# A greedy planner's allowances: results counted later for the transfers that read them, and a margin of 0.44 for TensorE in place of 0.42

## The chip, the cores and the metric

The kernel runs on one core of one Trainium2 chip. Its time is the device time of one execution in microseconds (us). A core has five engines with a line of instructions each: TensorE (PE, with its weight loads listed apart as PEld), VectorE (DVE), ScalarE (ACT), GpSimdE (POOL) and SyncE (SP), which here issues every DMA transfer. An engine takes its instructions in the order in which they were issued and waits on semaphores for the others.

## What is computed

One step of a hybrid decoder layer for 1024 new tokens of a prompt and 8 sample tokens with states of their own, model width 1024:

```python
p = x @ w_in                                   # 9360 columns: GLA, RWKV-7 and gate parts
o_gla, S_gla = gla_chunked(q, k, v, log_a)     # 4 heads, 128 x 256 state
o_gla = rmsnorm(o_gla) * silu(g_a)
pr = p_rwkv + (prev - p_rwkv) * mu             # token shift
y, S_rwkv = rwkv7_scan(r, w, k, v, kk, a)      # 16 heads, 64 x 64 state, one step per token
o_rwkv = (groupnorm(y) + bonus) * silu(g_b)
m = sigmoid(gate_a) * (o_gla @ w_up_gla) + sigmoid(gate_b) * (o_rwkv @ w_up_rwkv)
y_out = layernorm(alpha * x + m @ w_out)
```

Outputs are y for both groups, the new GLA and RWKV states, and the last projected RWKV rows. All is float32; the large matmuls are made from a high and a low part of each operand, three products each.

## The kernel before

**Stages.** The tokens go in two passes of 512 (the 8 sample tokens ride with the first). In each pass every block of 128 columns of `w_in` is projected: eight blocks of 128 rows by three products, for one or two tiles of tokens. From these rows come four GLA heads (`gla_head`) and eight pairs of RWKV heads (`pair`: `front`, `back`, `turn`, `chain`, `norm`). A pair's `front` makes Gram matrices, stores parts of them to DRAM (`LD`), loads them back in another layout, solves triangular blocks on VectorE (tiles `X`), and stores and reloads the result (`XD`, `XT`, `Xs`). A pair's `chain` is serial over eight chunks: three small matmuls (`pch`) with copies and scaled additions between them, and one pair's chain starts only when the one before has ended. Late in the second pass the eight sample states (`rwkv_sample`, loads `row<-state_rwkv`, stores `rwkv_s<-row`) are worked through. Then come the up projections with the gates (stored before as `sg`, loaded again by `load_gates`, merged as `mg`), and the output projection with the layer norm.

**Weights.** `load_w` loads a half block (`wraw`), ScalarE casts the high part into `wb`, VectorE or GpSimdE subtracts the low part, and in the first pass the split tile is also stored to DRAM (`keep`, `w<-wb`), from where the second pass loads it (`wb<-w`). There are four `wb` tiles. In `load_w`'s `low`, the tile is handed to the matmuls (`self.ws.append`) after the store has been issued.

**The order of issue.** Nothing of the order is written by hand. The work is written as some dozens of generators (`Stream`s), each of which yields its operations one at a time. `Order.run` is a greedy planner that runs while the program is built: at each step it asks every stream for its next operation, estimates when that could start (`start`), takes off a priority by the kind of stream, and issues the operation with the smallest key. It keeps an account of each engine's time, of when each tile is ready and by which engine it was made, and of when it was last read. The program that results is fixed; at run time the engines follow it with semaphores. So the constants of the estimate change the order of instructions, and nothing else.

In `start`, an operation can begin when its engine is free and when each of its tiles is ready. If another engine made a tile, an allowance is added: `HOP` for the maker, and `SPARE` more if the reader is TensorE and the maker VectorE, ScalarE or GpSimdE. `HOP["D"]` is for tiles that a transfer filled. If the same engine made it, 0.13 us are added (not for TensorE). A transfer (engine "S") costs SyncE 0.48 us in the account; `transfer` gives its time in the DMA engines, bytes of all runs divided over 16 engines at 0.01 us and 46.5 ps per byte a run, and 1.7 us (1.2 to DRAM) until it has landed. Only one operation of a stream is open at a time, so a stream whose transfer is planned later goes on later.

Of the kernel before, what the change touches and what calls it, by code (L numbers as in the profile page):

```python
# [20 lines left out]
P = 128  # L21
D = 1024
# [39 lines left out]
OUT_AHEAD = 3  # L62


HOP = {"P": 0.2, "D": 1.7, "G": 0.14, "V": 0.15, "A": 0.14}

SWITCH = 0.115
HOLD = 0.11
# [1 line left out]

AGE = 0.5

SPARE = 0.42
BIAS = 0.1
ASIDE = 0.5

# [164 lines left out]
class Order:  # L241
# [89 lines left out]
    def start(self, op):  # L331

        best = None
        for eng, fn, cost in op.ways:
            free, t = self.time[eng] + (SWITCH if eng == "P" and op.tiles != self.tiles else 0.0), 0.0
            for x in (op.out, *op.ins):
                at, by = self.ready.get(x.tensor.name, (0.0, None))
                if eng == "S" and by == "D" and x is op.out:
                    continue
                if by != eng:  # L340
                    at += HOP.get(by, 0.0) + (SPARE if eng == "P" and by in ("V", "A", "G") else 0.0)
                elif eng != "P" and x is not op.out:
                    at += 0.13
                t = max(t, at)
            t = max(t, self.read.get(op.out.tensor.name, 0.0))
            if eng in op.port:
                free = max(free, self.port["G" if eng == "V" else "V"])
            late, t = free - t, max(t, free)
            if eng in "VA" and self.held(eng, op):
                cost += HOLD  # L350
            end = t + cost
            if len(op.ways) > 1:
                end += BIAS if eng == "V" and "A" in op.ways[0][0] else ASIDE if eng == "G" and "G" in op.port else 0.0
            if best is None or end < best[0]:
                best = end, t
                op.eng, op.fn, op.cost, op.late = eng, fn, cost, max(0.0, late)
        return best[1]
# [1441 lines left out]
```

## Time and profile before

| | |
|---|---|
| runs | 1514.95, 1516.04, 1519.06 us; median 1516.04 |
| profiled execution | 1520.49 us, span 1518.7 us |
| granted TensorE clock, mean | 0.997 |
| TensorE busy | 1481.2 us (98%) |
| VectorE, ScalarE, GpSimdE busy | 1125.9 (74%), 877.4 (58%), 94.5 (6%) |
| DMA | 330.58 MB, 69.7% of 16 engines' span |

The span is the time from the first to the last instruction in the trace. "Idle before, releaser" in the rows of the profile is how long an engine stood before an instruction and whose result ended that; a row of the waits has the total in us, the number of times and the longest. All instructions carry the line 219, where a helper records them, so they are told apart by the names of their tiles (`out<-in`). In the rows by stretches of time, each engine's busy time is followed by its number of instructions, then come the granted clock, the share of the DMA engines that was busy and GB/s.

### The profile page before, as it was taken

The page shows a single profiled execution, that of the slowest core. Times are in us where ns is not written, and L with a number is a line of the kernel's source. Part 1 is how long each engine was busy: PE and PEld are TensorE (multiplying, and loading weights), DVE is VectorE, ACT ScalarE, POOL GpSimd, SP SyncE. Part 2 cuts the span into 40 slices and gives each one's busy share as a digit, 9 for nine tenths or more (in the row PEclk, how much of TensorE's full clock was granted, in tenths as well). Part 3 has the DMA queues.
Part 4 walks back from the last instruction along what each step waited for, and adds up shares of the span by engine and source line. Part 5 has one row for each costly group of instructions (what it writes and reads, how often), then busy time and mean ns, then how long its engine had stood idle before and what let it go on. Part 6 is the DMA issues. An engine that isn't in the chain of part 4 may idle for free.

```text
span 1518.7 us, 31506 instructions
## 1 busy us (share of the span) xinstructions
PE 1481.2 (98%) x11352; PEld 1303.4 (86%) x11352; DVE 1125.9 (74%) x2570; ACT 877.4 (58%) x2209; POOL 94.5 (6%) x273
## 2 busy tenths in 40 slices
PE   8999999999999999999999999899999999999997
PEld 7999999999999998877878777778788899988786
DVE  5687789786986698669778888776765775665665
ACT  5666677675677577566664555456546645554310
POOL 1010000000110000001001010200000000000000
PEclk9999999999999999999999999999999999999999
DMA  8768977789768976586576557555764778697622
GB/s 305 259 226 263 308 259 220 221 245 308 238 210 251 309 249 218 175 245 178 162 199 209 148 164 234 170 142 176 200 194 127 217 241 260 238 312 252 208 84 83
DMA packets 252823, 330.58 MB, mean 218 GB/s; under 512 B 125011, under 2 KB 148700, under 8 KB 252668
## 3 DMA queue, kind: packets, MB, share of 16 engines
q1 hardware_dynamic: 252668, 328.58, 69.7%
q8 instruction: 90, 1.47, 0.4%
q14 instruction: 65, 0.53, 0.1%
HBM read 198.35 MB, written 118.61 MB: 209 GB/s over the span
## 4 chain that ended last, share of the span: by engine, by line
PE 74%; DVE 13%; DMA 6%; ACT 3%; issue 2%; SPq 1%; POOL 0%; POOLq 0%; DVEq 0%; ACTq 0%
PE proj L219 45%; PE big L219 16%; PE pY L219 8%; DVE row L219 6%; PE pch L219 5%; DVE X L219 3%; ACT row L219 2%; SPq L219 1%; DVE wide L219 1%; DMA row<-sg 1%; DMA wide<-LD 1%; DVE part L219 1%; DMA w<-wb 1%; DVE pair L219 1%; DMA row<-state_rwkv 0%
## 5 line engine op out<-in xcount | busy, mean ns | idle before, releaser
L219 PE MATMUL proj<-xh,wb 128*128 128x256 f32 (+3 forms) x3744 | 912.7, 328 | 1.1 <-DVE row L219 0.8
L219 PEld LDWEIGHTS proj<-xh,wb 128*128 128x128 f32 x3744 | 624.4, 189 | 46.5 <-issue 2.6
L219 PE MATMUL proj<-xl,wb 128*128 128x256 f32 (+3 forms) x1872 | 612.1, 327 | 0.0
L219 PEld LDWEIGHTS proj<-xl,wb 128*128 128x128 f32 x1872 | 353.8, 189 | 23.2 <-issue 1.9
L219 DVE TENSOR_TENSOR wb<-wraw,wb 128x512 fp32r<-128x512 f32 x208 | 141.9, 689 | 78.1 <-ACT wb L219 74.3
L219 ACT CAST wb<-wraw 128x512 fp32r<-128x512 f32 x210 | 129.9, 622 | 90.3 <-PE proj L219 41.1
L219 DVE TENSOR_TENSOR row<-row 128x512 f32<-128x512 f32 (+8 forms) x338 | 166.1, 501 | 15.3 <-DMA row<-state_rwkv 6.4
L219 ACT ACTIVATE row<-row 128x512 f32<-128x512 f32 (+3 forms) x229 | 138.6, 611 | 36.2 <-DVE row L219 17.7
L219 DVE SCALAR_TENSOR_TENSOR wide<-pch,pc,s0p 64x64 f32<-64x64 f32 x224 | 63.1, 281 | 51.9 <-PE pch L219 46.9
L219 PE MATMUL big<-row 128*128 128x128 f32 (+4 forms) x466 | 87.1, 322 | 9.0 <-DVE row L219 4.1
L219 ACT ACTIVATE row<-proj,omu 128x256 f32<-128x256 f32 (+1 forms) x99 | 54.2, 548 | 68.6 <-PE proj L219 67.6
L219 ACT COPY rh<-pch 128x128 f32<-128x128 f32 x118 | 31.4, 266 | 105.6 <-PE pch L219 104.3
L219 DVE TENSOR_REDUCE X<-X 128x54 f32<-128x162 f32 (+14 forms) x256 | 85.4, 334 | 6.4
L219 ACT ACTIVATE s0p<-wide,pc 64x64 f32<-64x64 f32 x256 | 88.9, 347 | 1.8
L219 POOL TENSOR_TENSOR row<-row 128x256 f32<-128x256 f32 (+6 forms) x47 | 42.5, 909 | 688.0 <-DVE row L219 435.6
L219 DVE SCALAR_TENSOR_TENSOR row<-proj,pv,row 128x255 f32<-128x255 f32 (+1 forms) x99 | 56.4, 570 | 35.3 <-ACT tail L219 25.4
L219 PEld LDWEIGHTS big<-row 128*128 128x128 f32 (+3 forms) x466 | 59.5, 178 | 21.1 <-ACT row L219 7.0
L219 DVE TENSOR_TENSOR X<-X,wide 128x108 f32<-128x108 f32 (+14 forms) x256 | 71.2, 278 | 6.6
L392 ACT ACT_TABLE_LOAD x58 | 74.4, 1283 | 1.0
L219 PE MATMUL big<-xh,wb 128*128 128x512 f32 (+2 forms) x272 | 69.2, 332 | 2.9 <-ACT wb L219 2.6
L219 ACT COPY row<-big 128x128 f32<-128x128 f32 (+5 forms) x145 | 43.3, 317 | 38.4 <-PE big L219 35.5
L219 PE MATMUL pY<-xh,wb 128*128 128x256 f32 (+2 forms) x256 | 63.2, 326 | 0.0
(269 smaller groups left out, 2324.8 us busy)
## 6 DMA issues: line engine op xcount, KB each, us to landing
w<-wb SPq DMA_DIRECT2D x146, 512.0 KB
wb<-w SPq DMA_DIRECT2D x146, 512.0 KB
wraw<-w_in SPq DMA_DIRECT2D x146, 256.0 KB
wide<-LD SPq DMA_DIRECT2D x64, 128.0 KB
wraw<-w_up_gla SPq DMA_DIRECT2D x32, 256.0 KB
wraw<-w_up_rwkv SPq DMA_DIRECT2D x32, 256.0 KB
sg<-row SPq DMA_DIRECT2D x16, 260.0 KB
row<-sg SPq DMA_DIRECT2D x16, 260.0 KB
```

Of the source, the lines that this page charges most:

```text
L219: ways.append((eng, lambda call=call: call(out, *args, **kw), price(eng, name, out, args, ins)))
L392: self.nc.scalar.preload_act_table_set(self.table)
```

## The change

Three constants of the planner's estimate. VectorE's hop is 0.14 in place of 0.15, TensorE's margin on results of other engines is 0.44 in place of 0.42, and a transfer now has such a margin too (`STORE`, 0.3) on tiles that VectorE, ScalarE or GpSimdE made. No operation is added, removed or altered.

```diff
-HOP = {"P": 0.2, "D": 1.7, "G": 0.14, "V": 0.15, "A": 0.14}
+HOP = {"P": 0.2, "D": 1.7, "G": 0.14, "V": 0.14, "A": 0.14}
...
-SPARE = 0.42
+SPARE = 0.44
+STORE = 0.3
 BIAS = 0.1
 ASIDE = 0.5
...
                 if by != eng:
-                    at += HOP.get(by, 0.0) + (SPARE if eng == "P" and by in ("V", "A", "G") else 0.0)
+                    at += HOP.get(by, 0.0) + (SPARE if eng == "P" and by in ("V", "A", "G") else STORE if eng == "S" and by in ("V", "A", "G") else 0.0)
                 elif eng != "P" and x is not op.out:
                     at += 0.13
                 t = max(t, at)
```

## The prediction

> **What bounds the kernel now.** I read the page first, then the busy time by stretches of 50 us, then the waits of TensorE and of the DMA queue, then the timeline at the places where TensorE stood longest.
>
> ```profile
> span 1518.7 us, 31506 instructions
> PE 1481.2 (98%) x11352; PEld 1303.4 (86%) x11352; DVE 1125.9 (74%) x2570; ACT 877.4 (58%) x2209; POOL 94.5 (6%) x273
> ```
>
> TensorE is busy for 1481.2 of 1518.7 us. Whatever the order of issue does, the matmuls are the same ones, so the whole sum that another order can win from idle time is 1518.7 − 1481.2 = 37.5 us, less what is idle at the two ends. The stretches show where it lies:
>
> ```profile
> core 0: us, PE busy (x) PEld busy (x) DVE busy (x) ACT busy (x) POOL busy (x), PEclk, DMA share, GB/s
> ...
> 750.00:800.00 50.00, 48.51 (x311) 38.93 (x310) 39.10 (x103) 30.68 (x71) 3.64 (x4) 1.00 0.78 226
> 800.00:850.00 50.00, 47.04 (x339) 37.76 (x338) 44.45 (x116) 20.96 (x63) 8.16 (x17) 1.00 0.59 167
> 850.00:900.00 50.00, 47.85 (x327) 38.27 (x328) 42.21 (x81) 33.08 (x84) 5.05 (x13) 1.00 0.56 162
> 900.00:950.00 50.00, 48.80 (x307) 39.17 (x305) 41.57 (x92) 26.70 (x59) 1.34 (x2) 1.00 0.77 228
> 950.00:1000.00 50.00, 45.24 (x319) 36.52 (x320) 39.38 (x99) 20.25 (x62) 9.26 (x17) 0.97 0.59 167
> ...
> 1200.00:1250.00 50.00, 47.14 (x376) 43.91 (x375) 34.97 (x79) 27.45 (x53) 1.32 (x1) 0.97 0.76 230
> ...
> 1500.00:1518.70 18.70, 10.92 (x71) 9.74 (x69) 10.35 (x19) 0.99 (x4) 2.77 (x3) 0.92 0.17 61
> ```
>
> The last stretch loses 18.70 − 10.92 = 7.8 us in the closing normalisation, which has no other work beside it in any order. From 750 to 1000 us TensorE loses 250 − 237.44 = 12.6 us and around 1225 us another 2.9; only in the stretches that hold 950 and 1225 us is the granted clock below 1.00. Who ended these waits:
>
> ```profile
> PE pch L219 <- DVE wide L219: 4.6, 5, 2.0
> PE big L219 <- DVE row L219: 4.1, 6, 2.0
> PE big L219 <- DVE part L219: 3.5, 5, 1.4
> PE big L219 <- ACT wb L219: 2.6, 1, 2.6
> PE pch L219 <- ACT wide L219: 2.6, 3, 1.5
> ...
> PE proj L219 <- DVE wb L219: 0.2, 1, 0.2
> ```
>
> These are the first five and the last of 21 rows (total us, times, longest). All 21 add up to 28.9 us in 41 waits: 29 ended by VectorE, 10 by ScalarE, 2 by a transfer. They are the stock on which the change can work. The DMA queue's own waits:
>
> ```profile
> SPq L219 <- PE proj L219: 217.1, 100, 7.5
> SPq L219 <- DVE wb L219: 111.5, 80, 6.5
> SPq L219 <- DVE row L219: 88.1, 78, 5.5
> SPq L219 <- DVE X L219: 87.5, 53, 7.5
> ```
>
> SyncE issues every transfer in one line. It stands for 217.1/100 = 2.17 us at a time until matmuls let go of a buffer that a load will fill, and for 1.1 to 1.7 us at a time until VectorE has made what a store reads. Such time costs nothing by itself; it costs if a transfer that somebody needs is queued behind.
>
> **Part 1: TensorE's margin.** Nothing that runs is added or taken out; all three edits alter what the order of issue believes. For an operand made by VectorE the allowance becomes 0.14 + 0.44 = 0.58 in place of 0.15 + 0.42 = 0.57 us; made by ScalarE or GpSimdE, 0.58 in place of 0.56. A wait that a planned start 0.01 or 0.02 us later would shorten is shorter by just that: 29 × 0.01 + 10 × 0.02 = 0.5 us at most. On the other side, TensorE takes a projection matmul first a little more often, and a step of the serial chains is planned that much later. That costs nothing while projections fill the gap, which 98% busy says they do; without that cover the 16 pairs × 8 chunks × 3 matmul steps of the chain would be up to 384 × 0.02 = 7.7 us. I take −0.5.
>
> **Part 2: VectorE's hop.** ScalarE and GpSimdE now plan on VectorE's results 0.01 us sooner. ScalarE is 58% busy and GpSimdE 6%, so this prices at nothing; if ScalarE's order filled up it would be 0.01 us for each such operand, of which none shows among TensorE's waits. I take 0.
>
> **Part 3: the stores.** A transfer that reads a result of VectorE is planned 0.14 + 0.30 − 0.15 = 0.29 us later, one that reads ScalarE's or GpSimdE's 0.30. Two things follow: loads that are ready in that time are issued ahead of the store, and what follows the store (its landing, and the reads of what it wrote) is expected 0.3 us later, so more other work is put before it. The largest family is the copy of the split weights to DRAM in the first pass.
>
> ```profile
> L219 SPq DMA_DIRECT2D w<-wb x146: 320/448/1545, 6.5 to 580.0; - x146
> ```
>
> ```profile
> 126.86 1.47 PE proj L219 x12
> ```
>
> The stream that makes the weights hands a tile on only when this store has been issued, so in the planner's time each of 146 tiles is 0.29 us later. One tile feeds 24 matmuls, 24 × 1.47/12 = 2.9 us, and there are four tiles, so 11.8 us of matmuls hide it; the wait on this source in the table above is 0.2 us. With the cover gone it would be 146 × 0.29 = 42 us, and nothing in the first pass is near that. Zero.
>
> What can be won lies where a late transfer shows through to TensorE. I find three such places. The first is the start of the up projections:
>
> ```profile
> 1216.15 0.50 SPq L219 DMA_DIRECT2D row<-sg  x1
> ```
>
> ```profile
> 1222.14 0.64 ACT L219 ACTIVATE row<-row 128x520 f32<-128x520 f32 x1 [3.06 <-DMA row<-sg]
> ...
> 1230.36 0.39 PE L219 MATMUL big<-xh,wb 128*128 128x256 f32 x1 [2.64 <-ACT wb L219]
> ...
> 1231.09 0.51 PE L219 MATMUL big<-xh,wb 128*128 128x256 f32 x2 [0.22 <-DVE wb L219]
> ```
>
> The reader of a gate load starts 1222.14 − 1216.15 = 6.0 us after its issue, ScalarE idles 3.06 us for it with the casts of the next weights behind, and TensorE pays 2.64 + 0.22 = 2.86 us. The second and third are loads of the sample states:
>
> ```profile
> 943.37 0.69 DVE L219 TENSOR_TENSOR row<-row 128x512 f32<-128x512 f32 x1 [2.56 <-DMA row<-state_rwkv]
> ```
>
> ```profile
> 950.51 0.49 PE L219 MATMUL pch<-wide,gg 128*128 128x128 f32 x2 [1.51 <-ACT wide L219]
> 951.66 0.47 PE L219 MATMUL big<-part,headsr 128*128 128x512 f32 x1 [0.67 <-DVE part L219]
> ```
>
> ```profile
> 961.41 0.33 SPq L219 DMA_DIRECT2D row<-state_rwkv  x1
> ```
>
> ```profile
> 968.83 0.69 DVE L219 TENSOR_TENSOR row<-row 128x512 f32<-128x512 f32 x1 [3.82 <-DMA row<-state_rwkv]
> ```
>
> ```profile
> 971.02 0.46 PE L219 MATMUL pch<-wide,gg 128*128 128x128 f32 x2 [0.88 <-DVE wide L219]
> ...
> 978.13 0.46 PE L219 MATMUL pch<-wide,gg 128*128 128x128 f32 x2 [2.03 <-DVE wide L219]
> ```
>
> At 968.83 VectorE has stood 3.82 us in its own line, with the chain's scaled additions queued behind, and TensorE then pays 0.88 + 2.03 = 2.91 us (0.76 us for each us of VectorE); near 951 it pays 1.51 + 0.67 = 2.18. Two of the places also cost clock:
>
> ```profile
> 952.00:954.00 2.00, 2.00 (x24) 1.36 (x26) 2.00 (x5) 0.00 (x0) 0.00 (x0) 0.61 0.66 131
> 954.00:956.00 2.00, 2.00 (x48) 2.00 (x44) 1.97 (x5) 0.00 (x0) 0.54 (x1) 0.54 0.03 8
> ```
>
> ```profile
> 1232.00:1234.00 2.00, 2.00 (x13) 2.00 (x12) 1.94 (x6) 0.28 (x1) 0.00 (x0) 0.58 0.83 234
> 1234.00:1236.00 2.00, 2.00 (x12) 2.00 (x12) 1.86 (x7) 0.28 (x1) 0.00 (x0) 0.56 0.62 192
> ```
>
> The column after the engines is the granted clock: 2 × (0.39 + 0.46) = 1.7 us of full speed lost after the place near 951, 2 × (0.42 + 0.44) = 1.7 after the one near 1230. The three places together are worth 2.86 + 2.18 + 2.91 + 2 × 1.7 = 11.4 us.
>
> [...]
>
> How much of the 11.4 us does a margin of 0.3 us take? By the formulas of the code, the planner expects the state load at 0.48 to issue, 0.84 in the engines, 1.7 to land and 1.7 for the reader, 4.7 us; it took 968.83 − 961.41 = 7.4, and the 0.3 is put on stores, not on loads. If it reached these waits, it would cover about 0.3 of 2.56 to 3.82 us, a tenth: 1 us. The bounds are 11.4 us won, and on the other side as many new places as the reshuffle below can make. I take −1, by the ratio of the margin to those waits.
>
> **The sum.** The profiled execution took 1520.49 us (span 1518.7); the parts give −0.5 + 0 − 1 = −1.5, so 1519.0. It stands 4.45 us above the median of the runs, 1516.04; on the median the sum is 1514.5.
>
> **The reshuffle.** The order is greedy: as soon as one pick differs, the picks behind it differ, and the 41 waits are dealt again. The spread of such a deal follows from their sizes: the square root of the sum of squares is 5.8 us over the 41 rows of the timeline, from 2.64 down to 0.15 us, seven of which stand above. If both orders are such deals the difference has a spread of 1.41 × 5.8 = 8 us, larger than the sum itself. This is an estimate from the rows, and the weakest link of the forecast.
>
> **The rivals.** Forecast: the terms are what they are worth and the waits are dealt again at about the same total, 1514.5 us; within 0.3% (4.5 us of 1516.04, about what a measurement of this kernel can tell from no change). For it: the real sum of the edits is 0.01, 0.02 and 0.3 us against waits of 0.2 to 3.8 us.
>
> Faster: with stores planned later, the loads behind the 211 waits of the DMA queue in its last three rows above go out sooner, and the two places with a half clock behind them vanish without a successor: 2.86 + 2.18 + 2 × 1.7 = 8.4, with the 0.5 of the margin 8.9, so 1507.1 us. For it: all three places begin with a load that landed late. Against it: these loads are late by 3 us, not by 0.3.
>
> Slower: a store that another step needs (the grams to the solve, the solve's result to the chain) now falls behind a load that waits 2.17 us for matmuls, instead of ahead of it. It is then 2.17 − 0.30 = 1.87 us later than planned, VectorE stands in its line on the first step of the solve, and TensorE pays 0.76 × 1.87 = 1.4 us. The second pass has eight pairs with two such legs each; if five of sixteen are caught, it is 7.1 us less the 0.5, and on 1516.04 that gives 1522.6. It passes 0.3% from four on (4 × 1.4 = 5.7, less 0.5). For it: 100 such waits, and VectorE at 41.6 to 44.5 of 50 us in the stretches from 800 to 950 us. Against it: the planner keeps the line of SyncE in its account, so it sees most of this.
>
> **The numbers.** The forecast's case gets 0.43, faster by over 0.3% 0.36, slower by over 0.3% 0.21; the sum of −1.5 and the three places tilt it to faster. The spread of 8 us about 1514.5 holds 8 in 10 within 1.28 × 8 = 10.3 us; with some 1.5 to 2 us for the spread of the runs (1514.95 to 1519.06) I give 1502 to 1526, which takes in the whole 11.4 us on one side and eight caught stores (8 × 1.4 − 0.5 = 10.7) nearly on the other. The likeliest case alone runs from 1511.5 to 1520.6.
>
> **What would show it.** Right: the same matmul count, TensorE busy for 1481 ± 2 us, waits of TensorE that add up to 24 to 33 us at other places than before, the waits of the DMA queue on VectorE's weights, rows and X fewer or shorter. The faster rival shows as a granted clock of 1.00 in every stretch from 50 to 1500 us and no wait behind gate or state loads; the slower one as VectorE waiting on the solve's loads, with chain matmuls late behind it. The forecast is wrong if TensorE's waits halve or grow by half, or if the busy time itself moves by more than 3 us, for which I have no term.

## The result, and the profile after

The changed kernel took 1524.66 us (median of five runs, 1519.13 to 1528.45) against 1516.04 us: 1.0052 of before, interval 1.0037 to 1.0067. It is slower by about 8 us, on the side to which the prediction gave 0.21. The time lies inside the range on record, but the likeliest case was no change. One execution of null_s below took 5073.61 us and is left out of its numbers.

The page of the changed kernel first, then TensorE's waits, the DMA queue's waits and the stretches of 50 us, with the columns as before:

```profile
span 1521.1 us, 31519 instructions
## 1 busy us (share of the span) xinstructions
PE 1482.0 (97%) x11352; PEld 1303.0 (86%) x11352; DVE 1123.6 (74%) x2532; ACT 881.5 (58%) x2226; POOL 112.0 (7%) x292
```

```profile
PE big L220 <- DVE row L220: 4.1, 6, 2.0
PE big L220 <- DVE part L220: 4.0, 7, 0.8
PE pch L220 <- DVE wide L220: 3.1, 4, 1.1
...
PE proj L220 <- ACT wb L220: 2.3, 1, 2.3
...
PE big L220 <- DVE XT L220: 0.2, 1, 0.2
```

```profile
SPq L220 <- PE proj L220: 213.2, 104, 6.5
SPq L220 <- DVE wb L220: 136.3, 78, 6.5
SPq L220 <- DVE X L220: 82.4, 50, 4.4
SPq L220 <- DVE row L220: 74.1, 65, 7.5
```

```profile
250.00:300.00 50.00, 47.82 (x423) 44.99 (x423) 35.47 (x75) 34.23 (x88) 6.09 (x17) 0.97 0.59 186
300.00:350.00 50.00, 48.37 (x444) 45.82 (x443) 36.47 (x85) 33.51 (x80) 2.01 (x11) 0.97 0.83 264
...
950.00:1000.00 50.00, 49.35 (x310) 39.64 (x310) 43.24 (x101) 25.49 (x72) 8.46 (x18) 1.00 0.68 202
...
1200.00:1250.00 50.00, 50.00 (x408) 47.02 (x407) 37.91 (x85) 27.10 (x52) 0.00 (x0) 1.00 0.81 244
1250.00:1300.00 50.00, 46.46 (x393) 45.60 (x392) 23.38 (x48) 26.72 (x66) 2.61 (x2) 0.97 0.77 241
```

The instruction counts show that the constants do more than set the order: where an operation can run on more than one engine (`op.ways`), the planner takes the engine on which it expects the earlier end. So VectorE has 2532 instructions in place of 2570, ScalarE 2226 in place of 2209 and GpSimdE 292 in place of 273. That is part of what is called a deal below.

The same 11352 matmuls, the same busy time (1482.0 against 1481.2 us), nearly the same total of TensorE's waits: the rows add up to 29.4 us in 44 waits, against 28.9 in 41. But the waits are elsewhere. The stretch from 950 to 1000 us, which lost 4.8 us, now loses 0.65 at full clock, and the one from 1200 to 1250 loses nothing: the three places on which the prediction built its gain are gone. In their stead three others stand, each with the clock below 1.00. TensorE's rows at the three, from the timeline (the third place has two):

```profile
274.56 0.49 PE L220 MATMUL big<-row,S 128*128 128x128 f32 x2 [1.93 <-DVE S L220]
...
332.79 0.73 PE L220 MATMUL big<-Xs,As 128*64 128x32 f32 x14 [1.35 <-ACT As L220]
...
1264.01 0.38 PE L220 MATMUL proj<-xh,wb 128*128 128x256 f32 x1 [2.28 <-ACT wb L220]
...
1264.74 0.55 PE L220 MATMUL proj<-xh,wb 128*128 128x256 f32 x2 [0.23 <-DVE wb L220]
```

The one at 332.79 us lies in the first pass. The copy of `As` stood in ScalarE's line behind the cast of a weight whose load came late:

```profile
331.84 0.62 ACT L220 CAST wb<-wraw 128x512 fp32r<-128x512 f32 x1 [1.65 <-DMA wraw<-w_in]
```

The last one can be followed to the DMA queue (SyncE's line, then ScalarE's):

```profile
1242.85 0.38 SPq L220 DMA_DIRECT2D wraw<-w_up_gla  x1
...
1250.59 1.10 SPq L220 DMA_DIRECT2D row<-o_rwkv  x2
...
1252.49 2.88 SPq L220 DMA_DIRECT2D row<-o_rwkv  x6
1255.41 1.62 SPq L220 DMA_DIRECT2D gg<-az  x2
1257.13 1.15 SPq L220 DMA_DIRECT2D wraw<-w_up_gla  x2
```

```profile
1263.34 1.99 ACT L220 CAST wb<-wraw 128x512 fp32r<-128x512 f32 x3 [4.60 <-DMA wraw<-w_up_gla]
```

Two weight loads that the current up projection needs stand behind eight input loads of the next one; ScalarE waits 4.60 us for the first, and TensorE 2.28 us for the cast. In the kernel before, all of these weight loads went out ahead of the eight:

```profile
1252.12 0.43 SPq L219 DMA_DIRECT2D wraw<-w_up_gla  x1
...
1254.94 6.73 SPq L219 DMA_DIRECT2D row<-o_rwkv  x8
```

The cost of the place shows in two stretches with almost the same work, 140 projection matmuls (those that read a `wb` tile) from the 5500th on, with the others that run among them. Before, then after:

```profile
1249.30:1269.00 19.70, 19.70 (x186) 19.34 (x185) 8.24 (x16) 9.09 (x21) 0.00 (x0) 1.00 0.94 280
```

```profile
1246.40:1271.90 25.50, 21.96 (x187) 21.11 (x186) 8.71 (x17) 11.54 (x25) 0.00 (x0) 0.93 0.88 252
```

186 and 187 matmuls take 19.70 and 25.50 us: 3.5 us of it is idle, 0.07 × 25.5 = 1.8 us is clock.

The span of the profiled pair differs by only 2.4 us. A second profile of each kernel (below) makes it 5.4 in the means, still short of the 8 us of the timed runs.

### The profile page after: what moved, and what is told of

Read it like the earlier page. It is cut to its first block, busy times and chain, and to the rows that moved or that the text cites. A ratio compares the mean times of both kernels' runs of the same rounds, so it can differ in the third digit from the quotient of the medians.

```text
span 1521.1 us, 31519 instructions
## 1 busy us (share of the span) xinstructions
PE 1482.0 (97%) x11352; PEld 1303.0 (86%) x11352; DVE 1123.6 (74%) x2532; ACT 881.5 (58%) x2226; POOL 112.0 (7%) x292
## 4 chain that ended last, share of the span: by engine, by line
PE 68%; DVE 16%; ACT 6%; DMA 6%; issue 2%; SPq 2%; POOL 0%; POOLq 0%; DVEq 0%; ACTq 0%
PE proj L220 41%; PE big L220 15%; PE pY L220 7%; DVE row L220 7%; PE pch L220 4%; ACT row L220 3%; DVE X L220 3%; SPq L220 2%; DVE wide L220 2%; DMA wraw<-w_in 2%; DVE wb L220 1%; ACT L393 1%; DVE pair L220 1%; DVE part L220 1%; DMA row<-state_rwkv 0%
## 5 line engine op out<-in xcount | busy, mean ns | idle before, releaser
L220 PE MATMUL proj<-xh,wb 128*128 128x512 f32 (+3 forms) x3728 | 907.8, 328 | 3.6 <-ACT wb L220 2.3
L220 PE MATMUL proj<-xl,wb 128*128 128x512 f32 (+3 forms) x1864 | 612.4, 329 | 0.0
L220 DVE TENSOR_TENSOR row<-row 128x256 f32<-128x256 f32 (+8 forms) x323 | 161.5, 509 | 12.7 <-DMA row<-state_rwkv 3.3
L220 POOL TENSOR_TENSOR row<-row 128x256 f32<-128x256 f32 (+6 forms) x62 | 57.7, 933 | 652.2 <-DVE row L220 321.3
L220 ACT COPY row<-big 128x128 f32<-128x128 f32 (+6 forms) x146 | 43.4, 317 | 52.3 <-PE big L220 47.2
L220 PE MATMUL big<-xh,wb 128*128 128x256 f32 (+2 forms) x288 | 71.8, 328 | 0.0
L220 ACT COPY az<-pch 64x64 f32<-64x64 f32 x239 | 49.3, 206 | 25.5 <-PE pch L220 23.6
```

Source lines behind the costliest of these rows:

```text
L220: ways.append((eng, lambda call=call: call(out, *args, **kw), price(eng, name, out, args, ins)))
```

## The experiments

The theories, as the expectations call them. A: the waits are dealt again by any change of the order, whatever it means. B: the margin on transfers slows by itself; B2: TensorE's margin does; B3: only the three values together do; B4: the edits have effects that add up. C: waits and half-clock windows make all differences of the span. D: the loss is spread evenly over the transfers. E: late weights at the one place near 1260 us carry the loss.

**The parts alone.** The margin on transfers alone, and the two others alone, then each of those:

```diff
# store_only, against the kernel before
+STORE = 0.3      (and its use in start)
# margin_only
-HOP = {..., "V": 0.15, ...}    -SPARE = 0.42
+HOP = {..., "V": 0.14, ...}    +SPARE = 0.44
# spare_only: the second line of margin_only; hop_only: the first
```

> Only the 0.3 us margin on transfers; TensorE's margin 0.42 and VectorE's hop 0.15 as before. Theory A (the waits are dealt again, whatever the edit means): anywhere in 1516 +- 8 us, and this run and margin_only do not add up to the +8.6 us of the whole change. Theory B (the store margin itself is what slows): about 1524 us, +8, while margin_only stays at 1515.5. Theory C (half-clock windows behind single waits): time above before goes with the mean granted clock, 1.7 us for each 0.0011 of it.

> Only TensorE's margin 0.44 and VectorE's hop 0.14; no margin on transfers. Theory A: anywhere in 1516 +- 8 us. Theory B: 1515.5 us (the -0.5 of the prediction). A rival B2 (the margin delays the serial chains): about 1524 us here, and store_only at 1516.

> Before with TensorE's margin 0.44 alone. Theory A: another deal, anywhere in 1518 +- 8 us. Theory B4 (the edits have effects that add up): with hop_only it gives what margin_only gave, -0.24% of before in the sum of the two.

> Before with VectorE's hop 0.14 alone. Theory A: another deal, anywhere in 1518 +- 8 us. Theory B4: with spare_only it adds up to the -0.24% of margin_only; VectorE's results planned 0.01 us sooner should be worth 0.3 us at most by themselves (29 waits).

Measured: store_only 1515.04 us, 0.9991 (0.998 to 1.0003); margin_only 1513.41, 0.9976 (0.9961 to 0.9991); spare_only 1517.24, 1.0001 (0.9991 to 1.0012); hop_only 1517.93, 1.0014 (1.0003 to 1.0026). B and B2 fall: neither half slows. The halves give −0.09 and −0.24%, the whole +0.52; TensorE's margin and the hop give +0.01 and +0.14, both together −0.24. Nothing adds up, and B4 falls too.

**Edits without meaning.** One thousandth in a constant, in the kernel before and in the changed one:

```diff
# null_s, before            # null_h, before
-SPARE = 0.42               -HOLD = 0.11
+SPARE = 0.421              +HOLD = 0.111
# after_null_s, after       # after_null_h, after
-SPARE = 0.44               -HOLD = 0.11
+SPARE = 0.441              +HOLD = 0.111
```

> The kernel before with SPARE 0.421 in place of 0.42, an edit too small to mean anything: 0.001 us on each operand. It deals the order again from some point on. Theory A: differs from before by several us, either way (spread 6 to 8 us over such edits). Theories B and B2: within 2 us of 1516.

> The kernel before with HOLD 0.111 in place of 0.11, another edit without meaning, in the price of VectorE and ScalarE. Theory A: differs from before by several us, either way, and from null_s too. Theories B and B2: within 2 us of 1516.

> The changed kernel with SPARE 0.441 in place of 0.44, which deals the order of the changed kernel again from early on. Theory A: the slowness isn't tied to the three values together, so this lands anywhere in 1518 +- 8 us, likelier below 1522 than above. Theory B3 (each half is harmless, but the three values together are what slows): 1524 +- 2 us here and in after_null_h.

> The changed kernel with HOLD 0.111 in place of 0.11, the edit that cost the kernel before 8 us. Theory A: anywhere in 1518 +- 8 us, unrelated to what the same edit did to before. Theory B3: 1524 +- 2 us. A theory A2, that HOLD 0.111 is itself bad: 1524 or more.

Measured: null_s 1516.98 us, 1.0005 (0.999 to 1.0019); null_h 1524.70, 1.0054 (1.0034 to 1.0074); after_null_s 1523.63, 1.0039 (1.0024 to 1.0055); after_null_h 1518.07, 1.0006 (0.9994 to 1.0018). A change of 0.001 us in a price that has nothing to do with transfers makes the kernel before as slow as the change under study, and the same 0.001 us in the changed kernel takes nearly all of its loss away. B3 and A2 fall, A stands. A allows 8 us either way, so what supports it is less its own hits than null_h, after_null_h and the fall of the others. TensorE's rows of null_h show it losing its time near the same stage, but in another way:

```profile
1269.09 0.49 PE L219 MATMUL pch<-wide,gg 128*128 128x128 f32 x2 [3.41 <-ACT wide L219]
...
1271.06 0.80 PE L219 MATMUL pch<-rh,XT 128*128 128x128 f32 x2 [1.49 <-DVE wb L219]
```

Its weight loads stand ahead of the input loads as in the kernel before; here the chain's matmuls wait for a ScalarE that has a row of casts in front.

**Second profiles.** Both kernels again, with nothing changed.

> The kernel before, unchanged, with a profile of its own. All theories: the same time as before, ratio 1.000 within the interval of a run pair; the profile of this execution is expected nearer to the median than the first one, which took 1520.5 us. Theory C (waits and half-clock windows make the whole difference): span less the waits of TensorE less 1.7 us for each half-clock window is 1486 to 1488 us, as in the six profiles so far.

> The changed kernel, unchanged, with a second profile. All theories: 1.005 of before again. Theory C: its waits of TensorE plus 1.7 us for each half-clock window are 6 to 9 us above those of before_again, and the rest, 1486 to 1488 us, is the same.

Measured: 1517.99 us, 1.0004 (0.9988 to 1.002), and 1524.76 us, 1.0054 (1.0037 to 1.007). The longest waits come back at the same places in the second profiles; TensorE's rows of before_again, then of after_again:

```profile
950.69 0.49 PE L219 MATMUL pch<-wide,gg 128*128 128x128 f32 x2 [1.39 <-ACT wide L219]
...
976.95 0.46 PE L219 MATMUL pch<-wide,gg 128*128 128x128 f32 x2 [1.85 <-DVE wide L219]
...
1228.29 0.39 PE L219 MATMUL big<-xh,wb 128*128 128x256 f32 x1 [1.58 <-ACT wb L219]
```

```profile
275.83 0.49 PE L220 MATMUL big<-row,S 128*128 128x128 f32 x2 [1.92 <-DVE S L220]
...
333.92 0.65 PE L220 MATMUL big<-Xs,As 128*64 128x32 f32 x14 [1.44 <-ACT As L220]
...
1267.27 0.58 PE L220 MATMUL proj<-xh,wb 128*128 128x256 f32 x1 [3.32 <-ACT wb L220]
```

So the places belong to the order, and their size varies from one execution to the next (2.64 and 1.58 us near 1229, 2.28 and 3.32 near 1265).

The spans also show where the difference lies. From the 5500th projection matmul to the end the changed kernel takes 274.7 and 276.7 us (the second starts there at 1248.5 us), the kernel before 269.4 and 269.7 (the second at 1247.1): 6.1 us more in the means. Up to that matmul the changed kernel is 0.7 us ahead, so there the places gone and the places new come out even.

For theory C, this table has, for every profile of this study, the span, TensorE's waits (sum of the waits' rows), the number of 3.4 us windows at half clock ahead of the closing one, and what is left of the span after the waits and 1.7 us for each window:

| profile | span | waits | windows | rest |
|---|---|---|---|---|
| before / before_again | 1518.7 / 1516.8 | 28.9 / 28.3 | 2 / 1 | 1486.4 / 1486.8 |
| after / after_again | 1521.1 / 1525.2 | 29.4 / 30.4 | 3 / 4 | 1486.6 / 1488.0 |
| store_only | 1512.8 | 25.0 | 0 | 1487.8 |
| margin_only | 1513.9 | 23.4 | 2 | 1487.1 |
| spare_only | 1515.4 | 25.7 | 2 | 1486.3 |
| hop_only | 1518.9 | 25.3 | 0 | 1493.6 |
| null_s | 1515.8 | 24.1 | 3 | 1486.6 |
| null_h | 1523.9 | 31.6 | 3 | 1487.2 |
| after_null_s | 1521.3 | 30.2 | 3 | 1486.0 |
| after_null_h | 1518.5 | 27.7 | 2 | 1487.4 |
| sw_late | 1526.3 | 33.4 | 3 | 1487.8 |
| sw_225 | 1526.8 | 32.3 | 3 | 1489.4 |
| after_w | 1521.8 | 30.4 | 2 | 1488.0 |
| before_x | 1525.2 | 32.6 | 4 | 1485.8 |
| sw_late_w | 1528.7 | 33.6 | 4 | 1488.3 |
| sw_225_w | 1522.0 | 30.8 | 2 | 1487.8 |
| store_09 | 1516.0 | 23.8 | 2 | 1488.8 |
| margin_again | 1516.4 | 25.6 | 0 | 1490.8 |

The span varies by 16 us (1512.8 to 1528.7), the rest by 5, hop_only apart, and in 17 of the 20 by 3. So waits and windows account for most of the differences of the span. hop_only's other 6 us are busy time: 1485.1 us on its page without one half-clock window, against 1478.6 in store_only; why its matmuls took longer stays open. As it was put first, that the time goes with the mean clock, C fails: the runs of store_09 (below) have a mean granted clock of about 0.996, like those of the changed kernel, and are 5 us faster. In the means of the two profiles each, the changed kernel's 5.4 us are 1.3 of waits, 3.4 of clock (3.5 windows against 1.5) and 0.7 of rest. store_only, the shortest profile, has no half-clock window ahead of the closing one. Its page and its clock:

```profile
span 1512.8 us, 31579 instructions
...
PE 1478.6 (98%) x11352; PEld 1301.4 (86%) x11352; DVE 1128.6 (75%) x2573; ACT 882.0 (58%) x2199; POOL 112.9 (7%) x288
```

```profile
core 0: 1512.8 us, clock 0.999
```

**The constants switched midway.** The changed constants hold up to a point of the planner's time for TensorE, those of before from there:

```diff
# sw_late; sw_225 has 225.0
+SWITCH_AT = 1150.0
...
+            if self.time["P"] > SWITCH_AT and SPARE != 0.42:
+                SPARE, STORE, HOP = 0.42, 0.0, dict(HOP, V=0.15)
```

> The changed constants until the planner's time for TensorE is 1150 us, those of before from there: TensorE's order is that of the changed kernel up to 1223 us of its trace, and dealt again behind. Theory A with C (the time is lost at single places, each a wait and mostly a half-clock window): the places at 275 and 333 us stay with their windows, the one at 1264 to 1267 (2.5 to 3.3 us of waits and 1.7 to 3.4 of clock) is gone, so 1518 to 1521 us if no new place of that size turns up behind 1223. A theory D (the loss is spread evenly, a little on each transfer): five sixths of the loss stay, 1523 us, and the waits at 1264 don't matter.

> The same with the constants of before from 225 us of the planner's time: the changed order up to 245 us of its trace, dealt again behind. Theory A with C: no window at 275 and 333 by necessity; any time in 1518 +- 8 us, and span less waits less 1.7 us a window again 1486 to 1488. Theory D: a sixth of the loss, 1517 us. Theory B or B3 (the values slow the kernel for as long as they hold): 1517 us as well.

Measured: sw_late 1529.60 us, 1.0083 (1.0069 to 1.0097); sw_225 1526.40, 1.0068 (1.0052 to 1.0085). Both are slower than the changed kernel. sw_late shares its order up to 1223 us and lost more behind it, so the expectation of a gain there was wrong, and D, which wanted 1523, as well; sw_225 held the changed constants for a sixth of the time only, and is slow. sw_225's rest in the table, 1489.4 us, lies above the 1486 to 1488 that C wanted. Both again lose much of their time in the 140 matmuls from the 5500th on (29.0 and 28.2 us). That led to theory E.

**The order of the loads held.** after_w (and sw_late_w, sw_225_w in the same way) plans the eight input loads only after the 16 weight loads of `w_up_gla` of the first pass; before_x plans the last two weight loads only after the eight:

```diff
# after_w; self.ups counts the weight loads of w_up_gla in the first pass
-self.swap(self.o_rwkv, c.i, lambda c=c: c.rwkv_done == NPAIR and self.sampled)
+self.swap(self.o_rwkv, c.i, lambda c=c: c.rwkv_done == NPAIR and self.sampled and (c.i or self.ups == 16))
# before_x, ahead of each weight load; self.orw counts the row<-o_rwkv of the first pass
+yield lambda: src is not self.a['w_up_gla'] or i or self.ups < 14 or self.orw == NK
```

> The changed kernel, with one thing held: the eight loads of the RWKV results for the first pass (row<-o_rwkv) are planned only when all 16 weight loads of w_up_gla of that pass have been. Its order is the changed kernel's up to there; in the changed kernel two of those weight loads stand behind the eight. Theory E (the change lost its time because these weights came late, at one place): from the 5500th projection matmul on it takes 269 to 271 us like the faster kernels, in place of 274.7 and 276.7, and the time is 1518 to 1519 us, 1.001 to 1.002 of before. Theory A (only the dealing counts, everywhere): anywhere in 1520 +- 8 us.

> The kernel before with the opposite held: the last two weight loads of w_up_gla of the first pass are planned only after the eight row<-o_rwkv. Theory E: the loss of the change appears in the kernel before, 274 to 277 us from the 5500th projection matmul on in place of 269.5, the cast of the late weights waits 4 to 6 us for its load, and the time is 1521 to 1524 us, 1.0035 to 1.005 of before. Theory A: anywhere in 1516 +- 8 us.

> sw_late (1529.6 us) with the row<-o_rwkv loads held behind the weight loads; one weight load stood behind them. Theory E: the stretch from the 5500th projection matmul falls from 280.8 to 269 to 272 us and the time to 1518 to 1521 us. Theory A: no reason to fall; 1522 to 1530 us.

> sw_225 (1526.4 us) with the same held; one weight load stood behind. Theory E: the stretch falls from 281.4 to 269 to 272 us and the time to 1515 to 1518 us. Theory A: 1518 to 1530 us.

Measured: after_w 1522.71 us, 1.0034 (1.0022 to 1.0047); before_x 1517.79, 1.0002 (0.9989 to 1.0014); sw_late_w 1529.46, 1.0081 (1.0062 to 1.01); sw_225_w 1523.82, 1.0041 (1.0022 to 1.006). In after_w the place shrinks, from 25.5 to 22.0 us:

```profile
1248.00:1270.00 22.00, 20.03 (x186) 19.60 (x185) 5.84 (x11) 8.23 (x19) 0.00 (x0) 1.00 0.90 265
```

But the whole gains only some 2 to 3 us of the 8, with intervals that overlap those of the changed kernel. From the 5500th matmul to the end E wanted 269 to 272 us; the profiles of after_w, sw_late_w and sw_225_w show 273.8, 280.4 and 279.2. In before_x the loss was made on purpose and shows in its profile, first ScalarE, then TensorE:

```profile
1268.10 1.29 ACT L219 CAST wb<-wraw 128x512 fp32r<-128x512 f32 x2 [4.93 <-DMA wraw<-w_up_gla]
```

```profile
1268.77 0.39 PE L219 MATMUL proj<-xh,wb 128*128 128x256 f32 x1 [1.80 <-ACT wb L219]
```

Yet its median hardly moves: this profiled execution took 1526.97 us, the longest of its runs, against a median of 1517.79. Part of that length lies where the order is still that of the kernel before: near 484 us ScalarE waited 4.19 us for a load (`row<-vd`), 1.66 in before, and two half-clock windows follow from 488.40 us, which neither profile of before has there. sw_late_w gains nothing, sw_225_w 2.6 us by the medians and 4 by the ratios. All four edits also deal the order again behind the place, so none of them changes the place alone.

Two of the edits without meaning speak against E as well. after_null_h, which is as fast as before, has a weight load behind the eight input loads too (SyncE's line, then ScalarE's):

```profile
1252.20 3.22 SPq L220 DMA_DIRECT2D row<-o_rwkv  x5
...
1257.19 0.56 SPq L220 DMA_DIRECT2D wraw<-w_up_gla  x1
```

```profile
1263.90 1.18 ACT L220 CAST wb<-wraw 128x512 fp32r<-128x512 f32 x2 [5.25 <-DMA wraw<-w_up_gla]
```

ScalarE waits longer for it than in the changed kernel, 5.25 us, and TensorE stands only 0.2 us for the tile. after_null_s, which is slow, has all of these weight loads ahead of the eight. E falls as the cause of the whole: TensorE stood 0.2 us for a late weight load in after_null_h and 2.28 us in the changed kernel, and in after_null_s its longest waits from 1245 to 1282 us are 2.5 and 1.0 us for tiles of VectorE, none for a weight.

**A dose, and the fastest order again.**

```diff
# store_09, against the changed kernel; margin_again is margin_only
-STORE = 0.3
+STORE = 0.9
```

> The changed kernel with three times the margin on transfers, 0.9 in place of 0.3. Theory B (a transfer planned later is what costs): three times the loss, about 1540 us. Theory A (another deal): 1520 +- 8 us like the other orders.

> margin_only once more, TensorE's margin 0.44 and VectorE's hop 0.14 without the margin on transfers, the fastest order so far (0.9976 of before). If it is faster than both kernels, 0.996 to 0.999 again; if it was the luck of the first runs, 1.000.

Measured: store_09 1519.36 us, 1.0014 (1.0004 to 1.0025), less than the 0.3 us margin "cost", so B falls by its size too. margin_again 1514.13, 0.9975 (0.9963 to 0.9986): the change without the margin on transfers is 0.25% faster than before, and that repeats. It is faster than both kernels of this study. It is the same program both times, so the repeat shows that this order is fast; that the values are good is not shown, and neither of them is faster alone.

## Why the prediction was wrong

**Parts 1 to 3**, the direct effects (−0.5, 0 and −1 us), are too small to be checked here: neither a part alone nor three times the margin shows an effect that exceeds the differences between edits without meaning, so they are neither confirmed nor refuted. The five orders with a margin on transfers (store_only, after, after_null_s, after_null_h, store_09) average +0.20% of before, the five without (margin_only, spare_only, hop_only, null_s, null_h) +0.10%; with a spread of 0.26% among the ten, that tells nothing apart.

**The three places** were real, and the change did remove them, which the forecast had put down to the faster rival. What failed is that rival's "without a successor": 274, 333 and 1264 us succeeded, with three half-clock windows for two. One of them, 333 us, is a late weight load in the first pass, which Part 3 put at zero; that the margin on the stores made it late is not shown.

**The step that failed** is the term for the new deal, which the sum puts at nothing: "the waits are dealt again at about the same total". It measured about +8 us. The waits themselves did come out at about the same total, 29.4 and 30.4 us against 28.9 and 28.3. What the step left out is that a new deal brings half-clock windows of its own. The prediction counts lost clock only as something to win at the old places (2 × 1.7 us), and its spread of 5.8 us is worked out from the waits alone. The profiles have 3.5 windows after and 1.5 before in the means, 3.4 of their 5.4 us. Such windows stand in TensorE's busy time, 1485.1 against 1480.0 us in the second profiles (three windows more, 3 × 1.7 = 5.1), for which the prediction says that it has no term. Its other signs of being right held in the first profile, save that the waits of the DMA queue on VectorE's weights were about as many (78 for 80) and longer (136.3 for 111.5 us in total). So those signs could not tell a lucky deal from an unlucky one.

**The deal itself**, called the weakest link, was right in kind: the ten orders that differ from the kernel before by constants alone have a spread of 0.26%, 4 us, where the prediction had 5.8 us for one order. The change drew one of the two worst, and which way a single deal falls could not be read from this profile; in this the forecast had bad luck. The ten average 0.15% above the kernel before, and seven of them are at 1.0005 or more, which suggests that the kernel before is a better deal than most. With ten orders the standard error of that mean is 0.08%, so it is not shown.

**The slower rival** named the right side and another mechanism: five of sixteen stores of the second pass caught behind loads that wait for matmuls, 7.1 us. Its sign was VectorE waiting on the solve's loads. Before, then after:

```profile
DVE X L219 <- DMA wide<-LD: 3.7, 3, 1.8
```

```profile
DVE Xs L220 <- DMA Xs<-XD: 2.1, 1, 2.1
DVE X L220 <- DMA wide<-LD: 1.6, 1, 1.6
DVE wb L220 <- DMA wide<-LD: 0.7, 1, 0.7
```

That is 3.7 us in three waits and 4.4 in three. What was caught at 1264 us is a weight load behind input loads that SyncE issued without standing for matmuls, and holding those back gained 2 to 3 us in after_w and nothing in sw_late_w. The DMA queue's waits on VectorE's rows and X shrank.

**A slip** of the prediction changes nothing: its own table has the closing stretch below full clock as well (0.92).

**Still open**: the two pairs of profiles differ by 2.4 and 8.4 us, 5.4 in the means, where the medians of the timed runs differ by some 8. In those runs the mean granted clock is 0.9958 and 0.9961 for the changed kernel and 0.9970 to 0.9973 in the four later groups of runs of before (the first group has one stray record of 0.947), which is some 0.0012 × 1520 = 1.8 us. The other 6 us are waits or longer busy time, and how much each place costs on average would need many profiles of each kernel. hop_only's 6 us outside waits and windows weren't explained.

## What to carry to other kernels

Where a greedy planner writes the order, a constant is judged against edits that mean nothing: run the kernel with a thousandth more in some price, a few times over, and take their spread (here 0.26%) as the noise of any tuning step, which is wider than the interval of one measurement. A cause read from one pair of profiles, however well it fits, is to be made on purpose in the kernel before; here the fitting cause moved the time by 0.02%, with an interval of 0.9989 to 1.0014. Look also among the runs already made for one that has the suspected cause and is fast: here after_null_h.

## What the runs showed of the hardware

In the changed kernel a wait of 1.35 us, at 332.79 us, was followed by half clock for 3.41 us, and in the two first profiles such windows lie on a grid. In that of the changed kernel they begin at 275.19, 333.21 and 1265.05 us, 58.03 and 931.84 us apart, 17 and 273 times 3.413; in that of the kernel before they begin at 952.44 and 1232.33 us, 279.89 us apart, 82 times 3.413. The rows show the last 3.41 us of the grid ahead of a window. The changed kernel near 333 us, then the kernel before ahead of its window at 1232.33 us, then a stretch of it with no half clock behind; the granted clock is third from the end:

```profile
329.80:333.21 3.41, 1.78 (x22) 1.33 (x21) 2.10 (x5) 1.71 (x5) 0.00 (x0) 1.00 1.00 360
333.21:336.63 3.42, 3.42 (x22) 2.26 (x20) 2.15 (x4) 1.94 (x7) 0.00 (x0) 0.50 1.02 304
```

```profile
1228.92:1232.33 3.41, 1.75 (x12) 1.54 (x13) 3.31 (x9) 2.46 (x5) 0.00 (x0) 1.00 0.69 182
```

```profile
976.33:979.75 3.42, 1.62 (x10) 1.43 (x10) 3.08 (x11) 1.45 (x5) 0.00 (x0) 1.00 0.41 146
```

At a granted clock of 0.50, 3.41 us cost 1.7 us of full speed. Ahead of the five windows of the two first profiles TensorE was busy for 0.90 to 1.78 of 3.41 us, so it was idle for about half of the stretch or more; the longest single wait ahead of the window at 333.21 us was 1.35 us. The busy time sets no sharp limit in these rows: the stretch from 976.33 us, with 1.62 us busy, had full clock behind it (1.00 from 979.75 to 983.16 us). In the kernel before, the wait of 2.03 us at 978.13 had no window, and 2.64 us at 1230.36 had one, as the 1.35 us of the changed kernel had: length alone doesn't decide. Why the same order has two windows in the first profile of the kernel before and one in the second isn't shown.
